# First token group's transposes moved from the second output projection to the third, its operands to the fourth, and the second norm's row scaling moved to GpSimd

## The chip, the cores and the metric

The kernel runs on one core of a Trainium2 chip. The metric is the device time of one execution in microseconds (us), as the median of several runs; lower is better. A core has a matrix engine (TensorE, called PE), a vector engine (DVE), a scalar engine (ACT), GpSimd (POOL) and an engine that here only issues transfers (SP). Each runs its own list of instructions in order, and they wait for one another by semaphores. Sixteen DMA engines carry the transfers.

## The reference

One layer of a decoder: 2048 tokens (T), width 1024 (D), float32.

```python
u = rmsnorm(h, attn_pre_norm)
proj = u @ w_in                                   # 1024 -> 3584 columns, for two groups of heads
o_hg = rmsnorm(hgrn2_mix(q, f, i, lb)) * silu(g)  # gated linear recurrence, 4 heads
o_sb = rmsnorm(stick_breaking_mix(q, k, v))       # causal attention, 8 heads
mix = concatenate([o_hg, o_sb]) @ w_out           # the output projection
h = h + rmsnorm(mix, attn_post_norm)
u = rmsnorm(h, ffn_pre_norm)
gate, up = split(u @ w_gate_up)
h = h + rmsnorm((silu(gate) * up) @ w_down, ffn_post_norm)
h = h + (p @ ple_proj) * sigmoid(h @ ple_gate)
```

`rmsnorm` divides each row (token) by the root of its mean square and multiplies by a gain for each column.

## The kernel before

The tokens are worked in four groups of 512 (`NG`, `GT`), each four blocks of 128 (`TT`, `P`). Every matrix product is done in three passes of a rounded float32 type: an operand is split into a high part (a cast on ACT, L209 for weights, L811 for the FFN) and a low part (a subtraction on DVE or POOL, L210 and L812), and the passes are the lines L223, L224 and L225. The names are `wr` for a raw operand as loaded, `wh` and `wl` for a weight's parts, `uh` and `ul` for the other operand's.

First comes the input projection, under which attention and the recurrence of earlier groups are worked; they end during the second output projection. Attention turns its weights on PE into the PSUM bank "tr" (L443), and DVE and ACT split them (`ah`, `al`, L446, L448); the recurrence multiplies small blocks into the bank "hg" (L525 and others), for which POOL prepares `qp` (L562).

Then come four output projections, `out_proj(0)` to `out_proj(3)`, one for each token group: 32 steps of 12 matmuls, two steps a slot, so that `half` is 8 slots. ACT (L671) and DVE (L673) bring the result into `mix` tiles. `post_mix(g)` follows under the next projection: for each block of 128 tokens it scales `mix` by its norm and gain (L697, DVE), adds the input (L698, POOL), stores the sum `h` (L699), takes the second norm (squares on ACT, L269; row sums and power on POOL, L271, L272, L275), scales the rows by it (L702) and stores them as `un_s[g]` (L703). Then `turn(un_s[g], u_s[g], ...)` transposes this group: it loads tiles `xt` of 128x512 (L730), turns eight groups of four 128x128 blocks on PE into bank "tr" (L745), empties the bank on ACT with the gain into an `ev` buffer (L751), and stores that (L752). The `mix` tiles and the turned tiles share one pool of `ev` buffers, the tiles `xt`, `h` and `gb` one of `xt` buffers.

`first_operands` loads eight turned tiles from `u_s[0]` (L796), and splits them (L811, L812) for the first products of the FFN, which `Drive` runs after the fourth projection.

PE's order is the order in which the program is written: `weave` steps a main stream and, in proportion to its steps, streams beside it. The order on the other engines is chosen when the kernel is built, by a scheduler; the chip keeps to it. All loads and stores are issued by SP, in its order, so what stands behind a transfer that waits, waits too. At most eight transfers are on their way, since a transfer's semaphore is taken again after eight.

Of the kernel before, what the change touches and what calls it, by code (L numbers as in the profile page):

```python
# [12 lines left out]
AF = mybir.ActivationFunctionType  # L13
ALU = mybir.AluOpType
# [4 lines left out]
ND = D // P  # L19
GT = 512  # L20
NG = T // GT
TT = GT // P
# [26 lines left out]
def weave(main, slots, *subs):  # L49
    done = [0] * len(subs)  # L50
    for i in range(2 * slots):
        for k, (sub, total, phase) in enumerate(subs):
            if phase is None or i % 2 == phase:
                due = (i + 1) * total if phase is None else 2 * (i // 2 + 1) * total
                while done[k] * 2 * slots < due:
                    sub.step()
                    done[k] += 1
        main.step()
# [30 lines left out]
def hybrid_block(  # L89
# [6 lines left out]
    nc = tc.nc  # L96
# [8 lines left out]
    def scratch(name, shape):  # L105
        return [dram.tile(list(shape), F32, tag=f"{name}{g}", name=f"{name}{g}") for g in range(NG)]
# [10 lines left out]
    un_s = scratch("un_s", (GT, D))  # L117
    u_s = scratch("u_s", (ND, P, GT))
# [28 lines left out]
    def column(name, src, n):  # L147
        t = ctile(name, (P, n))
        nc.sync.dma_start(t, src.rearrange("(c p) -> p c", p=P))
        return t  # L150

    g_pre = column("g_pre", attn_pre_norm[0], ND)
    g_ffn = column("g_ffn", ffn_pre_norm[0], ND)
# [19 lines left out]
    def bank(tag):  # L173
        return ps.tile([P, 512], F32, tag=tag, name=tag, bufs=BANKS[tag])
# [15 lines left out]
    def xt(name="xt"):  # L190
        return fb.tile([P, GT], F32, tag="xt", name=name, bufs=8)
# [73 lines left out]
    def row_rstd(halves, out=None, ss=None):  # L265
        if ss is None:
            ss = const.tile([P, 2], F32, tag="ss", name="ss", bufs=8)
            for j, y in enumerate(halves):
                nc.scalar.activation(junk, y, AF.Square, accum_out=ss[:, j:j + 1])  # L269
        r = const.tile([P, 1], F32, tag="ssum", name="ssum", bufs=8)  # L270
        nc.gpsimd.tensor_tensor(r, ss[:, 0:1], ss[:, 1:2], op=ALU.add)  # L271
        nc.gpsimd.tensor_scalar(r, r, 1.0 / D, EPS, op0=ALU.mult, op1=ALU.add)  # L272
        if out is None:
            out = const.tile([P, 1], F32, tag="rstd2", name="rstd2", bufs=6)
        nc.gpsimd.tensor_tensor(out, r, neghalf, op=ALU.pow)  # L275
        return out
# [409 lines left out]
    def post_mix(g, mix):  # L686
        gb = [xt("gb") for _ in range(2)]
        for j in range(2):
            nc.sync.dma_start(gb[j], attn_post_norm[0:1][:, j * GT:(j + 1) * GT].to_broadcast((P, GT)))
        for t in range(TT):  # L690
            hs = [xt("h"), xt("h")]
            for j in range(2):
                nc.sync.dma_start(hs[j], x[g * GT + t * P:g * GT + (t + 1) * P, j * GT:(j + 1) * GT])
            r = row_rstd(mix[t])
            for j in range(2):
                d = mix[t][j]
                nc.vector.scalar_tensor_tensor(d, d, r, gb[j], op0=ALU.mult, op1=ALU.mult)  # L697
                nc.gpsimd.tensor_tensor(hs[j], hs[j], d, op=ALU.add)  # L698
                nc.sync.dma_start(h_s[g][t * P:(t + 1) * P, j * GT:(j + 1) * GT], hs[j])  # L699
            r = row_rstd(hs)  # L700
            for j in range(2):
                nc.scalar.activation(mix[t][j], hs[j], AF.Copy, scale=r)  # L702
                nc.sync.dma_start(un_s[g][t * P:(t + 1) * P, j * GT:(j + 1) * GT], mix[t][j])  # L703
            yield

# [17 lines left out]
    def turn(src, dst, gain, tag, new_in, new_out, scales=None):  # L723

        def get(q):
            ts = []
            for i in range(2):
                r = new_in().rearrange("p (t d) -> p t d", t=2)
                rows = src[2 * i * P:2 * (i + 1) * P, q * 256:(q + 1) * 256]
                nc.sync.dma_start(r, rows.rearrange("(t p) d -> p t d", p=P))  # L730
                for n in range(2):
                    if scales:
                        nc.scalar.activation(r[:, n, :], r[:, n, :], AF.Copy, scale=scales[2 * i + n])
                    ts.append(r[:, n, :])
            return ts

        nxt = get(0)
        yield
        for q in range(4):
            ts = nxt  # L740
            nxt = get(q + 1) if q < 3 else None
            for c in range(2):
                b = bank(tag)
                for t in range(TT):
                    nc.tensor.transpose(b[:, t * P:(t + 1) * P], ts[t][:, c * P:(c + 1) * P], ident)  # L745
                e = new_out()
                k = 2 * q + c
                if gain is None:
                    nc.scalar.copy(e, b)
                else:  # L750
                    nc.scalar.activation(e, b, AF.Copy, scale=gain[:, k:k + 1])  # L751
                nc.sync.dma_start(dst[k], e)  # L752
                yield
# [475 lines left out]
    rates = Rate(att_stream, 2, todo, 2 * OP_SLOTS)  # L1229
    r2 = Rate(hgs[2], 1, HG_STEPS - 42, 2)  # L1230
    r3 = Rate(hgs[3], 1, HG_STEPS, 2 * OP_SLOTS - 2)
    half = OP_SLOTS // 2
    tt0, tt1, ss0, ss1 = {}, {}, {}, {}

    def first_operands():
        for prod in (1, 2):
            for k in range(ND // 2):
                t_first(0, tt0, prod, k)
                yield

    for g in range(NG - 1):
        if g + 1 < NG - 1:
            out_load(g + 1, res[g + 1])
        op = Stream(out_proj(g, res[g]))
        if g == 0:
            weave(op, 2, rates.part(2), r2.part(2))
            hgs[2].drain()
            weave(op, OP_SLOTS - 2, rates.part(OP_SLOTS - 2), r3.part(OP_SLOTS - 2))
        elif g == 1:
            weave(op, half, rates.part(half), r3.part(half), (pm, TT, 0))  # L1250
            tu = Stream(turn(un_s[0], u_s[0], g_ffn, "tr", xt, ev))
            weave(op, half, rates.part(half), r3.part(half), (tu, 9, 0))
            hgs[3].drain()
            att_stream.drain()
            side.close()
            big[0] = ctx.enter_context(tc.tile_pool(name="bigr", bufs=1, side="right"))
            mm_tags[:] = ["mm", "z", "mm", "z", "mm", "av"]
        else:
            out_load(NG - 1, res[NG - 1])
            weave(op, half, (pm, TT, 0))  # L1260
            weave(op, half, (Stream(first_operands()), ND, 1))
        op.drain()
        pm = Stream(post_mix(g, res[g]["mix"]))

# [2 lines left out]
    drive.prepare(2)  # L1267
    op = Stream(out_proj(NG - 1, res[NG - 1]))
    tu = Stream(turn(un_s[1], u_s[1], g_ffn, "tr", xt, ev))
    weave(op, half + 2, (pm, TT, 0), (tu, 9, 0))  # L1270

    def third_operands():
        for k in range(ND // 2):
# [75 lines left out]
```

## Time and profile before

| | |
|---|---|
| median of 3 runs | 3080.39 us (3078.42 to 3082.84) |
| the profiled execution | 3079.93 us |
| its span | 3078.1 us |
| granted clock of PE, mean | 0.987 |
| PE busy | 2928.8 us, 95% of the span |
| DVE, ACT, POOL busy | 2042.8, 1580.6, 1603.7 us |
| output projections two to four | 1263 to 1497 us of the span |

An engine's row gives its busy time, its share of the span and its instructions. Where an instruction waited, a row of the timeline ends with the idle time before it and with what released it. A row of the waits sums these: total us, how often, the longest. "issue" stands where the profile shows no releaser. In a row of the transfers stand their count, their size and the median time from issue to landing.

### The profile page before, as it was taken

How to read it: one execution, taken by the hardware profiler on the slowest of the kernel's cores; microseconds unless marked ns; L12 is line 12 of the kernel's file. 1: busy time of each engine (PE TensorE's matmuls, PEld its weight loads, DVE VectorE, ACT ScalarE, POOL GpSimd, SP SyncE). 2: the span in 40 equal slices, each digit the busy share in tenths (PEclk: the TensorE clock that was granted, in tenths of full speed). 3: DMA queues.
4: the chain of work that ended last, by engine and by line, in shares of the span. 5: the costliest groups of instructions: out<-in, count | busy, mean ns of one | idle time of the engine just before them, and what ended most of it. 6: DMA issues, size and time to landing. Idle time of an engine off the chain costs nothing. (4 is left out here: it accounts for less than half of the span.)

```text
span 3078.1 us, 52969 instructions
## 1 busy us (share of the span) xinstructions
PE 2928.8 (95%) x18280; PEld 2429.9 (79%) x18280; DVE 2042.8 (66%) x2809; ACT 1580.6 (51%) x3188; POOL 1603.7 (52%) x1598
## 2 busy tenths in 40 slices
PE   8999999999999998888998999999899999999989
PEld 7888787878787877778776877788788888887767
DVE  3556566677767776745877766856687766656674
ACT  5666656666667666757523233445432323545442
POOL 3344455545556666857454544645634343556564
PEclk9999999999999999999999999999999999999999
DMA  7765565555444443457767767766955555677874
GB/s 216 217 211 164 157 185 158 148 156 162 141 140 150 147 144 122 164 176 264 253 212 245 238 214 236 234 198 218 328 179 171 172 170 175 209 225 251 286 246 144
DMA packets 469421, 602.29 MB, mean 196 GB/s; under 512 B 43168, under 2 KB 277664, under 8 KB 469152
## 3 DMA queue, kind: packets, MB, share of 16 engines
q1 hardware_dynamic: 469152, 598.91, 61.4%
q8 instruction: 144, 2.36, 0.3%
q14 instruction: 125, 1.02, 0.1%
HBM read 439.89 MB, written 158.86 MB: 195 GB/s over the span
## 5 line engine op out<-in xcount | busy, mean ns | idle before, releaser
L811 ACT CAST wh<-wr 128x512 fp32r<-128x512 f32 x600 | 352.3, 618 | 511.1 <-PE mm L224 139.0
L812 POOL TENSOR_TENSOR wl<-wr,wh 128x512 fp32r<-128x512 f32 x256 | 368.7, 1447 | 386.3 <-ACT wh L811 366.8
L435 POOL TENSOR_TENSOR a<-be,ring 128x512 f32<-128x512 f32 (+2 forms) x320 | 318.4, 995 | 434.5 <-DVE ring L431 418.3
L223 PE MATMUL mm<-uh,wh 128*128 128x512 f32 x1168 | 484.5, 415 | 5.2 <-DVE vv L350 3.2
L225 PE MATMUL mm<-uh,wl 128*128 128x512 f32 x1168 | 460.6, 394 | 0.0
L224 PE MATMUL mm<-ul,wh 128*128 128x512 f32 x1168 | 459.0, 393 | 1.6 <-DVE ul L812 1.6
L812 DVE TENSOR_TENSOR wl<-wr,wh 128x512 fp32r<-128x512 f32 x344 | 308.9, 902 | 204.4 <-ACT wh L811 177.6
L431 DVE TENSOR_TENSOR_SCAN ring<-z,ring,be 128x512 f32<-128x512 f32 x192 | 245.6, 1279 | 113.4 <-ACT z L417 110.0
L223 PE MATMUL mm<-wh,uh 128*128 128x256 f32 (+1 forms) x992 | 308.6, 311 | 0.0
L224 PE MATMUL mm<-wl,uh 128*128 128x256 f32 (+1 forms) x992 | 293.4, 296 | 1.6 <-DVE wl L812 1.3
L225 PE MATMUL mm<-wh,ul 128*128 128x256 f32 (+1 forms) x992 | 292.9, 295 | 0.0
L225 PEld LDWEIGHTS mm<-uh,wl 128*128 128x128 f32 x1168 | 220.5, 189 | 51.0
L223 PEld LDWEIGHTS mm<-uh,wh 128*128 128x128 f32 x1168 | 221.4, 190 | 47.6 <-issue 3.3
L224 PEld LDWEIGHTS mm<-ul,wh 128*128 128x128 f32 x1168 | 221.9, 190 | 41.7 <-DVE ul L812 2.0
L448 DVE TENSOR_TENSOR al<-tr,ah 128x512 fp32r<-128x512 f32 (+1 forms) x320 | 192.0, 600 | 90.1 <-ACT ah L446 89.4
L209 ACT CAST wh<-wr 128x512 fp32r<-128x512 f32 x288 | 178.2, 619 | 135.8 <-PE mm L224 81.5
L210 POOL TENSOR_TENSOR wl<-wr,wh 128x512 fp32r<-128x512 f32 x144 | 189.1, 1313 | 98.2 <-ACT wh L209 95.0
L446 ACT CAST ah<-tr 128x512 fp32r<-128x512 f32 (+1 forms) x320 | 167.6, 524 | 110.1 <-PE tr L443 107.1
L416 ACT ACTIVATE be<-z 128x512 f32<-128x512 f32 (+2 forms) x320 | 171.0, 534 | 90.5 <-PE z L410 38.3
L224 PEld LDWEIGHTS mm<-wl,uh 128*128 128x128 f32 x992 | 191.3, 193 | 8.0 <-DVE wl L812 1.7
L223 PEld LDWEIGHTS mm<-wh,uh 128*128 128x128 f32 x992 | 191.0, 193 | 8.1
L225 PEld LDWEIGHTS mm<-wh,ul 128*128 128x128 f32 x992 | 190.7, 192 | 4.3
(305 smaller groups left out, 7285.6 us busy)
## 6 DMA issues: line engine op xcount, KB each, us to landing
wr<-in_w_gate_up_dram SPq DMA_DIRECT2D x308, 256.0 KB, 3.4
wr<-in_w_in_dram SPq DMA_DIRECT2D x224, 256.0 KB, 3.1
wr<-hid_s SPq DMA_DIRECT2D x154, 256.0 KB, 3.1
wr<-in_w_down_dram SPq DMA_DIRECT2D x110, 256.0 KB, 3.3
hid_s<-hs SPq DMA_DIRECT2D x88, 256.0 KB, 2.7
wr<-wd_s SPq DMA_DIRECT2D x88, 256.0 KB, 3.1
kt<-k_s SPq DMA_DIRECT2D x80, 256.0 KB, 3.1
vt<-v_s SPq DMA_DIRECT2D x80, 256.0 KB, 3.3
```

The source lines that it names most:

```text
L209: nc.scalar.copy(hi, src)
L210: (lo_engine or nc.gpsimd).tensor_tensor(lo, src, hi.bitcast(F32), op=ALU.subtract)
L223: nc.tensor.matmul(o, l[0], r[0], start=start, stop=False)
L224: nc.tensor.matmul(o, l[0], r[1], start=False, stop=False)
L225: nc.tensor.matmul(o, l[1], r[0], start=False, stop=stop)
L416: nc.scalar.activation(be[:, :n], z[:, :n], AF.Sigmoid, scale=0.125)
L431: nc.vector.tensor_tensor_scan(r[:, o:o + n][:, ::-1], z[:, :n][:, ::-1], be[:, :n][:, ::-1], init, op0=ALU.mult, op1=ALU.bypass)
L435: nc.gpsimd.tensor_tensor(a[:, :n], be[:, :n], r[:, o + 1:o + n + 1], op=ALU.mult)
L446: nc.scalar.copy(hi[:, lo_c:], tr[:, lo_c:])
L448: nc.vector.tensor_tensor(lo[:, lo_c:], tr[:, lo_c:], hi[:, lo_c:].bitcast(F32), op=ALU.subtract)
L811: nc.scalar.copy(hi, src)
L812: lo_engine.tensor_tensor(lo, src, hi.bitcast(F32), op=ALU.subtract)
```

## The change

It does three things. The scaling of rows in `post_mix`, L702, goes from ACT to POOL (24 instructions of 128x512, in the groups 0 to 2). The first group's `turn` goes from the second half of the second projection to the second half of the third. `first_operands` goes from there to the first ten slots of the fourth projection, beside `post_mix(2)` and `turn(un_s[1])`.

```diff
             r = row_rstd(hs)
             for j in range(2):
-                nc.scalar.activation(mix[t][j], hs[j], AF.Copy, scale=r)
+                nc.gpsimd.tensor_scalar(mix[t][j], hs[j], r, None, op0=ALU.mult)
                 nc.sync.dma_start(un_s[g][t * P:(t + 1) * P, j * GT:(j + 1) * GT], mix[t][j])
...
         elif g == 1:
             weave(op, half, rates.part(half), r3.part(half), (pm, TT, 0))
-            tu = Stream(turn(un_s[0], u_s[0], g_ffn, "tr", xt, ev))
-            weave(op, half, rates.part(half), r3.part(half), (tu, 9, 0))
+            weave(op, half, rates.part(half), r3.part(half))
...
             weave(op, half, (pm, TT, 0))
-            weave(op, half, (Stream(first_operands()), ND, 1))
+            tu = Stream(turn(un_s[0], u_s[0], g_ffn, "tr", xt, ev))
+            weave(op, half, (tu, 9, 0))
...
-    weave(op, half + 2, (pm, TT, 0), (tu, 9, 0))
+    weave(op, half + 2, (pm, TT, 0), (tu, 9, 0), (Stream(first_operands()), ND, 1))
```

What this makes of the engines' lists is shown at three places. On POOL, in the first half of the second projection, before (`h` and `mix` are the tiles of `post_mix`, `rstd` the row scales, `qp` the recurrence's operand):

```order
862 L275 TENSOR_TENSOR rstd_17118<-ssum,neghalf 128x1
863 L698 TENSOR_TENSOR h<-h,mix 128x512
864 L562 TENSOR_TENSOR qp<-qp,tree 128x32x8
865 L698 TENSOR_TENSOR h<-h,mix 128x512
866 L210 TENSOR_TENSOR wl<-wr,wh 128x512
867 L271 TENSOR_TENSOR ssum<-ss 128x1
```

and after:

```order
862 L275 TENSOR_TENSOR rstd_17118<-ssum,neghalf 128x1
863 L702 TENSOR_SCALAR mix<-h,rstd_16927 128x512 x2
864 L698 TENSOR_TENSOR h<-h,mix 128x512 x2
865 L562 TENSOR_TENSOR qp<-qp,tree 128x32x8
866 L210 TENSOR_TENSOR wl<-wr,wh 128x512
867 L435 TENSOR_TENSOR a<-be,ring_217 128x512
```

A pair of scalings, and the second addition, now stand ahead of the `qp` product.

On SP, around the first group's turned tiles: before, their eight reloads stand together in the third projection's first half, all of the stores being long issued:

```order
910 L616 DMA tmp_18160<-o_s3_6_143 128x512
911 L796 DMA wr_18607<-u_s0_99 128x512
912 L796 DMA wr_18640<-u_s0_99 128x512
913 L796 DMA wr_18685<-u_s0_99 128x512
914 L796 DMA wr_18718<-u_s0_99 128x512
915 L796 DMA wr_18763<-u_s0_99 128x512
```

and after, in its second half (`un_s0` and `u_s0` are the first group's rows and turned tiles):

```order
918 L752 DMA u_s0_99<-ev_18511 128x512
919 L699 DMA h_s1_88<-h_18306 128x512
920 L699 DMA h_s1_88<-h_18307 128x512
921 L796 DMA wr_18947<-u_s0_99 128x512
922 L730 DMA xt_18502<-un_s0_95 128x2x256
923 L730 DMA xt_18504<-un_s0_95 128x2x256
924 L752 DMA u_s0_99<-ev_18562 128x512
925 L703 DMA un_s1_96<-mix_16705 128x512
926 L730 DMA xt_18592<-un_s0_95 128x2x256
927 L796 DMA wr_18992<-u_s0_99 128x512
```

Each reload (L796) now stands close behind the store that it reads (L752), and loads of `xt` stand behind it.

On ACT, in the third projection's second half, before:

```order
1841 L209 CAST wh_18818<-wr_18816 128x512
1842 L671 ACTIVATE mix_18578<-z_18750,rg_18215 128x256
1843 L671 ACTIVATE mix_18579<-z_18750,rg_18215 128x256
1844 L209 CAST wh_18824<-wr_18822 128x512
1845 L671 ACTIVATE mix_18580<-mm_18783,rg_18215 128x256
1846 L671 ACTIVATE mix_18581<-mm_18783,rg_18215 128x256
1847 L209 CAST wh_18972<-wr_18970 128x512
```

and after:

```order
1801 L751 ACTIVATE ev_18562<-tr_18557,g_ffn_172 128x512
1802 L811 CAST uh_18949<-wr_18947 128x512
1803 L209 CAST wh_18612<-wr_18610 128x512
1804 L209 CAST wh_18692<-wr_18690 128x512
1805 L671 ACTIVATE mix_18516<-mm_18565,rg_18135 128x256
1806 L671 ACTIVATE mix_18517<-mm_18565,rg_18135 128x256
1807 L811 CAST uh_18994<-wr_18992 128x512
1808 L751 ACTIVATE ev_18601<-tr_18596,g_ffn_172 128x512
1809 L269 ACTIVATE junk_204,ss_18420<-h_18402 128x512
1810 L209 CAST wh_18698<-wr_18696 128x512
```

Evictions (L751) and casts of reloaded operands (L811) now stand between the weight casts. Here `ev_18562` and `mix_18516` take buffers whose last contents went out with the store of the eviction just before, and wait until that has landed.

## The prediction

> **What bounds the kernel now.** I read the head of the page first, then the busy time by stretches, then what the TensorE (PE) waited for in each stretch, and last the timelines around those waits.
>
> ```profile
> span 3078.1 us, 52969 instructions
> PE 2928.8 (95%) x18280; PEld 2429.9 (79%) x18280; DVE 2042.8 (66%) x2809; ACT 1580.6 (51%) x3188; POOL 1603.7 (52%) x1598
> ```
>
> PE is busy for 95% of the span, so an edit counts only where PE idles or where it makes PE idle. The profiled execution took 3079.93 us, 1.83 us more than its span and 0.46 us below the median of 3080.39; my sum is made against 3079.93, and the median differs by less than can be told apart.
>
> The stretches are: first projection (1176:1250, for comparison), both halves of the second (1264:1313, 1313:1375), both halves of the third (1376:1403, 1403:1436), and the part of the fourth in which the second group is turned (1436:1470). Columns: length, busy time of each engine with its count, granted clock, DMA share, GB/s.
>
> ```profile
> 1176.00:1250.00 74.00, 71.13 (x906) 63.81 (x906) 50.99 (x82) 47.36 (x105) 45.89 (x56) 1.00 0.35 110
> 1264.00:1313.00 49.00, 40.50 (x466) 35.73 (x466) 34.84 (x51) 37.51 (x88) 43.31 (x56) 0.93 0.54 181
> 1313.00:1375.00 62.00, 51.18 (x575) 46.87 (x574) 27.98 (x48) 30.76 (x61) 29.66 (x34) 0.97 0.48 154
> 1376.00:1403.00 27.00, 22.64 (x180) 21.63 (x179) 21.33 (x24) 24.24 (x53) 23.06 (x25) 1.00 0.99 333
> 1403.00:1436.00 33.00, 29.43 (x231) 28.82 (x230) 18.89 (x25) 17.38 (x40) 21.74 (x25) 0.95 0.60 199
> 1436.00:1470.00 34.00, 29.47 (x242) 28.39 (x241) 13.18 (x20) 25.93 (x59) 23.50 (x31) 1.00 0.87 305
> ```
>
> PE idles 8.5 us of the 49, 10.8 of the 62, 4.4 of the 27, 3.6 of the 33 and 4.5 of the 34. What it waited for (total us, times, longest), in the same stretches:
>
> ```profile
> PE hg L525 <- POOL qp L562: 6.1, 2, 4.0
> ...
> PE tr L745 <- issue: 6.6, 3, 3.0
> PE tr L745 <- DVE al L448: 3.3, 2, 1.7
> ...
> PE tr L443 <- ACT ev L751: 0.2, 1, 0.2
> ...
> PE tr L745 <- ACT ev L751: 4.4, 3, 1.6
> ```
>
> So the transposes that the change moves (L745) hold 9.9 of the 10.8 us in the second projection's second half: they share the PSUM bank "tr" with attention's own transposes L443, and wait for that bank. In the first half the bound is POOL, 43.31 busy of 49. The same transposes in the fourth projection wait for ACT to empty the bank.
>
> **The change, term by term.**
>
> A. Second projection, second half: eight groups of L745 go. One group costs PE 0.35 us without a wait, from its start to that of the next matmul:
>
> ```profile
> 1357.38 0.60 PE L745 MATMUL tr<-ident,xt 128*128 128x128 f32 x4
> 1357.73 0.36 PE L223 MATMUL mm<-wh,uh 128*128 128x256 f32 x1
> ...
> 1358.05 0.28 PE L225 MATMUL mm<-wh,ul 128*128 128x256 f32 x1
> 1358.17 0.28 PE L223 MATMUL mm<-wh,uh 128*128 128x256 f32 x1
> ```
>
> Removed: waits 6.6 + 3.3 + 0.2 = 10.1, work 8 x 0.35 = 2.8, and about 1.0 of the slow clock (0.97 on 51 us of work is at most 1.5). Put back: with shorter cover, attention will hold PE as it does in the first projection, 2.87 idle of 74; on the 48 us that are left that is 1.9, against 0.7 of other idle time now, so +1.2. A = -12.7. ACT (30.76 less 8 evictions) and POOL (29.66) still fit into 48 us, so I put the ends at -14 and -8.
>
> B. Second projection, first half: POOL gets 8 scalings L702 of 128x512. POOL has not run this one; its nearest row is another TENSOR_SCALAR of that size, beside the ACT row that goes (least, median, most ns):
>
> ```profile
> L507 POOL TENSOR_SCALAR pd<-pd,oml,lb x16: 767/776/1209, 219.2 to 1282.6; 128x512 f32<-128x512 f32 x16
> ...
> L702 ACT ACTIVATE mix<-h,rstd x24: 705/720/757, 1272.9 to 1472.5; 128x512 f32<-128x512 f32 x24
> ```
>
> 8 x 0.78 = 6.2 us on an engine that has 5.7 idle and on which PE already waits. The pairs stand in POOL's queue right ahead of the qp products (L562) for which PE waits twice, so a pair, 1.55, is added to each: +3.1. Ends: 0, if POOL's idle time takes them, and +6.2, if all are in front of qp. ACT loses 5.8 of 37.51 there, but no long wait names it, so I count nothing.
>
> C. Third projection, first half: POOL gets another 6.2 on 23.06 of 27. But the first operands leave: eight loads, eight ACT casts L811 and eight DVE subtractions L812, which here run beside POOL and stretch it. Rows of DVE and of POOL:
>
> ```profile
> 1389.26 3.43 DVE L812 TENSOR_TENSOR ul<-wr,uh 128x512 fp32r<-128x512 f32 x2
> ...
> 1385.35 3.44 POOL L698 TENSOR_TENSOR h<-h,mix 128x512 f32<-128x512 f32 x2 [1.31 <-DVE mix L697]
> ...
> 1445.32 1.27 POOL L698 TENSOR_TENSOR h<-h,mix 128x512 f32<-128x512 f32 x1 [2.21 <-PE z L225]
> ```
>
> A POOL product takes 1.72 beside DVE and 1.27 alone. About four of POOL's products meet L812, so 4 x 0.45 = 1.8 comes back and POOL stands at 23.06 + 6.2 - 1.8 = 27.5 of 27: full, while ACT, DVE and the DMA (0.99) ease. C = +0.5, ends -3 (the easing wins) and +4.4 (6.2 - 1.8, all of it late).
>
> The Trainium skill ("SBUF — State Buffer", Terms) says that VectorE and GpSimd share one port pair by an exclusive lock, on which the loser stands fully blocked for the whole instruction; the rule speaks against moving work to POOL, and by it all 24 scalings could hold DVE or be held. The trace agrees in part: 1.72 against 1.27 is a loss of 0.45, not of a whole instruction. It gives the third rival below.
>
> D. Third projection, second half: eight groups of turn(un_s[0]) come in. Their bank is free of attention here, but ACT's order is now eviction, store, cast of a reloaded operand (L811), next eviction: most evictions take an `ev` buffer whose store must have landed first, five of them the store of an eviction just before. The half now lasts from 1402.79 to 1432.49, 29.7 us:
>
> ```profile
> 1402.79 0.28 PE L225 MATMUL mm<-wh,ul 128*128 128x256 f32 x1
> ...
> 1432.49 0.28 PE L225 MATMUL mm<-wh,ul 128*128 128x256 f32 x1
> 1408.84 0.58 PE L224 MATMUL z<-wl,uh 128*128 128x256 f32 x1 [2.81 <-POOL wl L210]
> 1416.80 0.39 PE L224 MATMUL av<-wl,uh 128*128 128x256 f32 x1 [0.68 <-POOL wl L210]
> ```
>
> If all of the turn were hidden it would last 29.7 + 2.8 - 3.5 (both waits hidden too) = 29.0. By the chain it lasts: 3.0 until the first xt load, which stands in SP's queue behind stores that now wait for POOL (estimate: a pair of L702 and half a landing), 8 evictions x 0.69 = 5.5, some four other ACT rows of 0.62 between them, 2.5, six landings in series, and after the last group 24 matmuls x 0.12 = 2.9. That is 13.9 + six landings. A landing of 256 KB (KB, median us), in 1320:1375, 1400:1436 and 1436:1470:
>
> ```profile
> u_s<-ev SPq DMA_DIRECT2D x8, 256.0 KB, 3.8
> ...
> h_s<-h SPq DMA_DIRECT2D x5, 256.0 KB, 3.0
> ...
> u_s<-ev SPq DMA_DIRECT2D x8, 256.0 KB, 5.2
> ...
> 1446.61 0.66 PE L745 MATMUL tr<-ident,xt 128*128 128x128 f32 x4 [1.30 <-ACT ev L751]
> ```
>
> With 3.8 it is 36.7, D = +7.0; with 3.0, 31.9 and +2.2; with 5.2, 45.1 and +15.4. I take 3.8: it is the same transfer, at a DMA share of 0.48, and the 0.60 of this half grows by some 20 transfers, while the queue, which stops at each store, keeps few in flight. In the fourth projection, where the buffers are two evictions apart, PE waits 4.4 for such a turn; here they are one apart. The ends are -0.7 and +15.4.
>
> The Trainium skill ("DMA: Bandwidth & Descriptors", Anatomy of one DMA) fits a transfer on the GpSimd path by 2.0 us and bytes over 436 GB/s; for 256 KB that is 2.6 (an estimate; these stores are issued by SP). By it D would be -0.2 and the whole sum -6.7. The medians above, 3.0 to 5.2, lie higher.
>
> E. Fourth projection: the last two operands' casts stand on ACT ahead of the weight cast (L209) of the second product, each behind a store and a reload, 2 x 3.8 = 7.6, of which one product of 3 us (24 matmuls) is cover: +4.6. Against it, eight L702 leave ACT (5.8 of 25.93), which should halve the 4.4 of waits for evictions: -2.0, estimated. E = +2.6, ends -3 and +6. The casts and subtractions that come here run on a DVE with 13.18 of 34 busy, so they are hidden. POOL, 23.50 + 6.2 of 34, stays under its length.
>
> Sum: -12.7 + 3.1 + 0.5 + 7.0 + 2.6 = +0.5, so 3079.93 + 0.5 = 3080.4.
>
> **The rivals.** First, the gain is kept. Landings at 2.6 to 3.0 hide the chain (D about +1), POOL's idle time takes half of the scalings (B +1.5), the eased DMA and ACT win in C (-1), E is 0: -12.7 + 1.5 - 1 + 1 = -11.2, 3069. For it: A rests on waits that are plainly in the rows, and 3.0 is what stores take in this very stretch. Against it: PE waits for just such evictions in the fourth projection.
>
> Second, slower: the chain through `ev` and DMA decides alone. If the added transfers fill the DMA as in 1436:1470 (share 0.87), a landing is 5.2, D = +15.4, E = +4.6: -12.7 + 3.1 + 0.5 + 15.4 + 4.6 = +10.9, 3091. It costs more than A gives from landings of about 4.7 on. For it: the same store at 5.2 one stretch later. Against it: a queue that waits for landings cannot keep the engines full.
>
> Third, slower by POOL: each scaling is stretched as L698 is, 0.78 + 0.45 = 1.23, 9.8 a half. Then the first halves run at POOL's length: B = 43.31 + 9.8 - 49 = 4.1, and the 3.1 for the order as well, C = 23.06 + 9.8 - 1.8 - 27 = 4.1: -12.7 + 7.2 + 4.1 + 7.0 + 2.6 = +8.2, 3088. For it: L507 once took 1.209. Against it: its median of 0.776, in stretches as busy as these.
>
> **How the numbers follow.** 0.2%, 6.2 us, is about what a measurement of this kernel can tell from no change. My forecast, within it, gets 0.38; the gain kept 0.34; the chain 0.18; POOL 0.10. So faster 0.34, same 0.38, slower 0.28. The likeliest alone spans 3074 to 3086; the range takes in the kept gain and the chain: 3067 to 3092.
>
> **What would show it.** Right: no L745 among the waits of the second projection's second half, which shrinks from 61 to about 48.5 us; L525 waiting for qp for over 6.1 us in its first half; L745 waiting for `ev` L751 for some 7 us or more in the third projection's second half, and that half at about 37 us; L702 on POOL at a median near 0.78. Wrong: a second half of the third projection at 30 us (then the first rival), landings there over 4.7 (the second), L702 near 1.2 (the third), or another stage that loses by more than 3 us, the FFN's start above all, for which I count nothing.

## Result, and the profile after

The changed kernel takes 3096.82 us (median of 6 runs, 3089.08 to 3100.52) against 3079.40 for the kernel before: ratio 1.0057, interval 1.0040 to 1.0073. It is slower by 0.57% and lies above the range of 3067 to 3092. The profiled execution took 3095.75 us. The head of its page:

```profile
span 3093.9 us, 52956 instructions
PE 2938.6 (95%) x18280; PEld 2438.3 (79%) x18280; DVE 2035.6 (66%) x2809; ACT 1569.5 (51%) x3164; POOL 1636.7 (53%) x1622
```

POOL gained 33 us of busy time, ACT lost 11: the 24 scalings cost POOL far more than the 18.7 us of the prediction. The stretches of the changed kernel are both halves of the second projection, the third projection up to one matmul of its second quarter (L224, at 1398.25 here and at 1399.69 before), its rest, and the fourth (length, busy time by engine, granted clock, DMA share, GB/s):

```profile
1266.10:1317.30 51.20, 39.47 (x457) 34.93 (x457) 33.54 (x51) 33.64 (x81) 49.64 (x56) 0.90 0.57 185
1317.30:1368.80 51.50, 48.97 (x550) 45.05 (x550) 27.99 (x48) 25.38 (x54) 33.06 (x40) 0.97 0.32 105
1368.80:1398.30 29.50, 22.43 (x167) 21.38 (x166) 16.55 (x20) 19.26 (x44) 28.12 (x28) 0.92 0.59 192
1398.30:1442.90 44.60, 36.00 (x259) 34.57 (x260) 15.27 (x24) 21.97 (x47) 24.20 (x26) 0.90 0.84 276
1442.90:1510.10 67.20, 55.90 (x427) 54.67 (x426) 32.52 (x48) 37.17 (x86) 46.77 (x54) 0.92 0.88 298
```

The kernel before, cut at the same instructions (the windows are rounded, by up to 0.4 us):

```profile
1263.00:1311.00 48.00, 39.53 (x456) 34.76 (x456) 33.53 (x51) 37.36 (x89) 42.97 (x55) 0.93 0.55 183
1311.00:1374.00 63.00, 51.80 (x577) 47.50 (x578) 28.58 (x50) 31.15 (x62) 29.68 (x35) 0.97 0.47 151
1374.00:1400.00 26.00, 21.64 (x172) 20.63 (x172) 20.93 (x24) 23.43 (x52) 23.09 (x24) 1.00 1.00 340
1400.00:1432.60 32.60, 29.03 (x227) 28.42 (x226) 17.88 (x25) 19.00 (x42) 20.93 (x26) 0.95 0.67 219
1432.60:1490.50 57.90, 52.34 (x427) 50.66 (x426) 29.75 (x45) 38.91 (x88) 31.04 (x39) 1.00 0.89 312
```

POOL is busy for 49.64 of 51.20 and 28.12 of 29.50 us in the first and third of these stretches: it is the bound there. The second projection's second half did shrink, by 11.5 us. The third and fourth projections give back 25: 13.5 of it is more idle time of PE, 2.8 the transposes that came in, and some 8.5 longer busy time of the same matmuls (114.3 us against 103.0, less the 2.8). The lower granted clocks explain nearly all of that: the busy time of before, rescaled stretch by stretch to the clocks of after, grows by 8.0. What PE waited for in the five stretches of the changed kernel:

```profile
PE hg L525 <- POOL qp L562: 8.9, 2, 7.2
...
PE hg L589 <- DVE sl L585: 2.2, 1, 2.2
...
PE z L224 <- POOL wl L210: 3.5, 2, 2.5
...
PE tr L745 <- ACT ev L751: 6.0, 3, 3.0
PE tr L745 <- DMA xt<-un_s: 2.5, 3, 1.3
...
PE z L224 <- POOL wl L210: 7.3, 3, 3.5
PE tr L745 <- DVE rg L643: 3.1, 1, 3.1
```

And the group of L702 (least, median, most ns):

```profile
L702 POOL TENSOR_SCALAR mix<-h,rstd x24: 1563/1576/2522, 1279.2 to 1496.2; 128x512 f32<-128x512 f32 x24
```

One scaling costs POOL 1.576 us, not 0.78, and no single one of the 24 took less than 1.563. How that meets PE is seen in the second projection's first half; rows of POOL's timeline, then of PE's:

```profile
1277.91 1.30 POOL L210 TENSOR_TENSOR wl<-wr,wh 128x512 fp32r<-128x512 f32 x1
1279.18 3.76 POOL L702 TENSOR_SCALAR mix<-h,rstd 128x512 f32<-128x512 f32 x2
1282.91 1.09 POOL L435 TENSOR_TENSOR a<-be,ring 128x512 f32<-128x512 f32 x1
1283.96 2.48 POOL L698 TENSOR_TENSOR h<-h,mix 128x512 f32<-128x512 f32 x2
1286.43 0.76 POOL L507 TENSOR_SCALAR pd<-pd,oml,lb 128x512 f32<-128x512 f32 x1
...
1287.95 0.66 PE L525 MATMUL hg<-qp,ks 128*32 128x32 f32 x32 [7.25 <-POOL qp L562]
```

PE waits from 1280.70 to 1287.95. The pair of scalings takes 3.76 us, 2.2 of them inside this wait; the rest of the wait is the rows behind it, up to the `qp` product. L507, the row from which the price was taken, takes 0.76 three rows on.

That pair ran beside work of DVE. In the rest of the third projection two scalings ran with DVE idle but for one row; POOL's row, then DVE's:

```profile
1412.46 3.13 POOL L702 TENSOR_SCALAR mix<-h,rstd 128x512 f32<-128x512 f32 x2
...
1414.92 0.69 DVE L812 TENSOR_TENSOR ul<-wr,uh 128x512 fp32r<-128x512 f32 x1 [6.88 <-ACT uh L811]
```

DVE sat idle for 6.88 us until 1414.92, so the first of the two, which ended at 1414.04, had nothing beside it and still took 1.58 us.

### The profile page after: what moved, and what is told of

Same layout as the page of the kernel before. It is cut to its first block, busy times and chain, and to the rows that moved or that the text cites. A ratio compares the mean times of both kernels' runs of the same rounds, so it can differ in the third digit from the quotient of the medians.

```text
span 3093.9 us, 52956 instructions
## 1 busy us (share of the span) xinstructions
PE 2938.6 (95%) x18280; PEld 2438.3 (79%) x18280; DVE 2035.6 (66%) x2809; ACT 1569.5 (51%) x3164; POOL 1636.7 (53%) x1622
## 3 DMA queue, kind: packets, MB, share of 16 engines
q1 hardware_dynamic: 469152, 598.91, 61.5%
## 5 line engine op out<-in xcount | busy, mean ns | idle before, releaser
L811 ACT CAST wh<-wr 128x512 fp32r<-128x512 f32 x600 | 352.5, 618 | 512.4 <-PE mm L224 135.6
L812 POOL TENSOR_TENSOR wl<-wr,wh 128x512 fp32r<-128x512 f32 x256 | 365.9, 1436 | 387.2 <-ACT wh L811 371.8
L224 PE MATMUL mm<-ul,wh 128*128 128x512 f32 x1168 | 459.8, 394 | 2.7 <-DVE ul L812 2.7
L812 DVE TENSOR_TENSOR wl<-wr,wh 128x512 fp32r<-128x512 f32 x344 | 310.8, 909 | 203.5 <-ACT wh L811 182.9
L224 PE MATMUL mm<-wl,uh 128*128 128x256 f32 (+1 forms) x992 | 295.1, 297 | 3.6 <-DVE wl L812 2.9
L224 PEld LDWEIGHTS mm<-ul,wh 128*128 128x128 f32 x1168 | 222.2, 190 | 42.9 <-DVE ul L812 3.1
L210 POOL TENSOR_TENSOR wl<-wr,wh 128x512 fp32r<-128x512 f32 x144 | 188.7, 1310 | 99.2 <-ACT wh L209 94.0
L224 PEld LDWEIGHTS mm<-wl,uh 128*128 128x128 f32 x992 | 193.1, 195 | 9.9 <-DVE wl L812 3.4
```

What stands on the lines that cost most here:

```text
L210: (lo_engine or nc.gpsimd).tensor_tensor(lo, src, hi.bitcast(F32), op=ALU.subtract)
L224: nc.tensor.matmul(o, l[0], r[1], start=False, stop=False)
L811: nc.scalar.copy(hi, src)
L812: lo_engine.tensor_tensor(lo, src, hi.bitcast(F32), op=ALU.subtract)
```

## Experiments

Lengths of the stages in each profiled execution, in us, cut at the L640 sums that open each projection, the first L589 of the recurrence's last head, the L224 of the third projection named above, the first matmul of the FFN, and the FFN's first long wait of L745. The last column is what comes after. Each row is one execution, up to 7 us off the median of its kernel, so differences of one or two us in a cell mean little.

| kernel | second, first half | second, second half | third, first part | third, rest | fourth | FFN's start | rest |
|---|---|---|---|---|---|---|---|
| before | 48.0 | 63.0 | 25.3 | 32.9 | 57.9 | 193.8 | 1393.8 |
| changed | 51.2 | 51.5 | 29.5 | 44.7 | 67.2 | 192.5 | 1391.3 |
| e1_moves | 48.0 | 48.4 | 30.9 | 34.9 | 64.9 | 191.1 | 1391.9 |
| e2_pool | 52.9 | 74.2 | 27.5 | 31.6 | 64.6 | 194.3 | 1392.4 |
| e3_two_ops | 53.4 | 48.4 | 29.4 | 38.5 | 62.2 | 191.6 | 1396.9 |
| e4_pool_two_ops | 53.3 | 63.9 | 30.2 | 33.7 | 61.7 | 191.1 | 1391.6 |
| e7_own_bank | 50.6 | 51.2 | 24.8 | 34.9 | 57.5 | 193.9 | 1392.2 |
| e10_both_acc | 49.1 | 48.3 | 31.7 | 32.1 | 57.2 | 1579.2 with the rest | |
| e13_counter | 48.1 | 48.4 | 30.9 | 35.8 | 64.2 | 190.6 | 1386.2 |
| e15_acc_no_count | 49.1 | 48.3 | 30.9 | 32.5 | 63.1 | 196.5 | 1388.8 |
| e16_late_weights | 47.9 | 48.3 | 25.2 | 40.0 | 66.3 | 190.6 | 1398.1 |
| e17_own_bank_late | 49.1 | 51.2 | 25.8 | 32.5 | 55.7 | 192.1 | 1384.0 |
| e18_changed_late | 52.4 | 49.9 | 25.4 | 44.4 | 64.9 | 195.0 | 1393.3 |

All ratios below are to the kernel before, run on the same chip.

### The two parts of the change, and the scaling's form

**The moves alone** (e1_moves):

```diff
-                nc.gpsimd.tensor_scalar(mix[t][j], hs[j], r, None, op0=ALU.mult)
+                nc.scalar.activation(mix[t][j], hs[j], AF.Copy, scale=r)
```

> The two moves alone: the second norm's scaling L702 is back on ACT, the transposes and the first operands stay where the change puts them. Theory P (POOL's price): the loss of the changed kernel comes from L702 costing POOL 1.576 us each instead of the 0.78 that I took, so without it the first halves of the second and third projections fall back to about 48 and 25 us, the fourth projection to about 60, and the time is 3066 to 3075, clearly under the kernel before. Theory R (round trips): the loss comes from the chain eviction, store, reload and cast; then the third projection's second half stays at about 44 us and the fourth at about 65, only some 7 us come back, and the time is 3084 to 3092.

Measured: 3078.56 us, ratio 0.9981 (0.9968 to 0.9995). The moves alone gain a little: 14.7 us in the second half of the second projection, of which the third and fourth take back 14.6 in this execution. Theory P's number was too low and theory R's too high; the sign is P's. Read against this row of the table, the scaling on POOL costs the changed kernel 3.2, 3.1, -1.4, 9.8 and 2.3 us in the five stages, 17.0 in all.

**The scaling alone** (e2_pool: the kernel before with the line of the change on POOL):

> The scaling alone: L702 on POOL, transposes and operands where they were before. Theory P: 24 x 1.576 = 38 us of POOL time fall into halves in which it is already full; the second projection's first half grows by 3, the third's first half by 4 or more (its first operands still run there), the fourth by 5 to 9; with the second half of the second projection unchanged the time is 3092 to 3102. Theory R: only the two first halves lose, 3 to 7 in all, and the time is 3082 to 3087.

Measured: 3098.63, ratio 1.0041 (1.0024 to 1.0059). Alone it loses about 13 us, so it is the scaling that makes the change slower. In the profiled execution, the slowest of the eight and 6 us above their median, 11 us of the loss lie where neither theory put them, in the second projection's second half: the transposes wait there for loads of the rows that POOL has scaled. The group, and PE's longest wait from the halves' border on:

```profile
L702 POOL TENSOR_SCALAR mix<-h,rstd x24: 1551/1572/2448, 1280.2 to 1508.1; 128x512 f32<-128x512 f32 x24
...
PE tr L745 <- DMA xt<-un_s: 6.4, 1, 6.4
```

**The changed kernel, scaling in two operations** (e3_two_ops):

```diff
-                nc.gpsimd.tensor_scalar(mix[t][j], hs[j], r, None, op0=ALU.mult)
+                nc.gpsimd.tensor_scalar(mix[t][j], hs[j], r, 1.0, op0=ALU.mult, op1=ALU.mult)
```

> The changed kernel with L702 written as two operations, times the row's scale and times 1.0, the form in which POOL's other scaling of this size, L507, took 0.776. If the form sets the price, L702 falls from 1.576 to about 0.78; theory P then expects 3066 to 3080, theory R 3086 to 3094. If L702 stays at 1.58, the price hangs on something else (input and output being different tiles, or neighbours), and the time stays at 3094 to 3100 by both.

Measured: 3085.03, ratio 1.0003 (0.9991 to 1.0015).

```profile
L702 POOL TENSOR_SCALAR mix<-h,rstd x24: 687/692/1380, 1281.3 to 1480.8; 128x512 f32<-128x512 f32 x24
```

A second operation, a multiplication by one, makes the instruction 2.3 times as fast: 0.692 against 1.576 us. The form sets the price. With it the loss against the kernel before is gone. Of the 0.76% by which the changed kernel stands above the moves alone, the form is 0.54, and 0.22 remain as the cost of the cheap form on POOL. Stage by stage the rest of the third projection is 6.2 and the fourth 5.0 shorter than in the changed kernel, the second half of the second 3.1; only its first half did not get shorter (53.4), at a granted clock of 0.84. The scheduler answered the new form with another order (41 of POOL's 1622 instructions stand elsewhere), so a part of the gain may be the order's; no run parts the two.

**The scaling alone, in two operations** (e4_pool_two_ops):

> The scaling alone, on POOL, as two operations; transposes and operands as before. If the price falls to 0.78, theory P expects half or less of the loss of the scaling alone, 3080 to 3088; theory R 3078 to 3084. If the price stays at 1.58, the time equals that of the scaling alone in one operation.

Measured: 3092.45, ratio 1.0026 (1.0014 to 1.0039), L702 at 0.692 at the median. Nearly two thirds of the loss remain at a price below that of ACT's 0.720, more than P expected, though the two intervals overlap. In the profiled execution the cheap form costs 5.3 us in the second projection's first half and 4.9 in the third's first part. In the whole third projection PE waits 11.8 us for low parts of weights from POOL (L210), against 6.4 before. POOL itself is busy for 47.7 of the 53.3 us of that first half, so it is late there without being full.

### Where the moves lose what they gain

**The operands later** (e5_late_operands: the moves alone, `first_operands` from the first ten slots of the fourth projection to its last six):

> The two moves alone (scaling on ACT), and the first operands still later: in the last six slots of the fourth projection, behind the second group's transposes. With the moves alone the third projection took 65.8 us and the fourth 64.9, against 58.2 and 57.9 before. Theory O (reloads and casts of the operands, waiting among the evictions, cost these 14.6 us): the third falls to 60 or less, the fourth to 60 or less unless the loads at its end hold the FFN back; time 3068 to 3075. Theory V (the evictions wait for buffers of `ev` whatever stands between them): both stay within 2 us, time 3076 to 3082.

Measured: 3078.62, ratio 0.9980 (0.9968 to 0.9991), third 67.7 and fourth 62.5. No change in the time: theory O falls.

**Tiles of their own** (e6_acc_tiles):

```diff
-            tu = Stream(turn(un_s[0], u_s[0], g_ffn, "tr", xt, ev))
+            tu = Stream(turn(un_s[0], u_s[0], g_ffn, "tr", xt, acc))
```

> The two moves alone, but the first group's turned tiles go to the FFN's `acc` buffers (two, used by nothing else there) instead of the pool that they share with the `mix` tiles. Theory V: evictions no longer wait for stores of `mix`, and two buffers take turns, so the third projection falls from 65.8 to about 61 and the fourth by a few; time 3068 to 3076. Theory O: the casts still wait for the reloads; third and fourth stay within 2 us, time 3076 to 3082.

Measured: 3066.55, ratio 0.9939 (0.9926 to 0.9951): the time that V expected, but not from where V expected it. The third projection took 64.7, the fourth 61.5, and what comes after the FFN's start 1384.8, against 65.8, 64.9 and 1391.9 with the moves alone. The edit had a second effect: `acc` deals its tiles to two pools by a counter, which eight tiles more leave at another place for the whole FFN. Two runs part the two effects.

**The counter alone** (e13_counter: the moves alone, with `turns["acc"] += 8` ahead of the FFN):

> The two moves alone (scaling on ACT), with the counter that deals the FFN's `acc` buffers to their two pools advanced by 8 before the FFN: buffers are given out in another order, all work is the same. If the counter is what gained after the FFN's start when the turned tiles went to `acc`, this gains about 4 to 6 on the moves alone (ratio to the kernel before 0.9960 to 0.9970, from 0.9981) and the third and fourth projection stay at 65.8 and 64.9. If the shared buffers are the cause, it stays at 0.998.

Measured: 3069.69, ratio 0.9964 (0.9952 to 0.9976).

**Tiles of their own, the counter set back** (e15_acc_no_count: `turns["acc"] -= 8` ahead of the FFN):

> The two moves with the first group's turned tiles in `acc`, the counter set back by 8 before the FFN, so that its buffers are dealt as in the kernel before. If the counter made the gain after the FFN's start, the FFN's start is as with the moves alone and the ratio 0.9955 to 0.9968; if the buffers did, 0.9939 again. Theory V for the third and fourth projection expects 64.7 and 61.5 us again.

Measured: 3075.14, ratio 0.9979 (0.9967 to 0.9991), third 63.4, fourth 63.1. The counter gains; buffers of their own, by themselves, gain nothing that shows in the time. The counter's gain lies in the FFN. From its first matmul to the end, the twelve kernels without the shift (the one before and the changed one among them) take 1582 to 1589 us in their profiled executions, the seven with a shift of 8 take 1566 to 1578. The shift changes the order of the engines' lists as well, so "counter" stands for both.

The two parts do not add up to the whole: 0.0017 and 0.0002 against 0.0042 for the tiles in `acc`. And theory V does not fall with the time: with the tiles in `acc` and the counter set back, the rest of the third projection and the fourth together are 4.2 us shorter than with the moves alone, but the FFN's start is 5.4 longer; its long wait of L745 is 16.0 us there, and 12.1 with the moves alone. Why is not shown.

**The FFN's weights later** (e16_late_weights: the moves alone, `drive.prepare(2)` moved behind the fourth projection's first ten slots). With the moves alone, 5.6 us are lost in the third projection's first part. PE's waits there, and POOL's rows ahead of the longest:

```profile
PE av L224 <- POOL wl L210: 5.4, 1, 5.4
...
1374.70 3.45 POOL L698 TENSOR_TENSOR h<-h,mix 128x512 f32<-128x512 f32 x2 [0.63 <-DVE mix L697]
1378.10 1.72 POOL L628 TENSOR_TENSOR oss<-oss,tmp 128x512 f32<-128x512 f32 x1
1379.78 1.72 POOL L812 TENSOR_TENSOR wl<-wr,wh 128x512 fp32r<-128x512 f32 x1
1381.46 1.71 POOL L210 TENSOR_TENSOR wl<-wr,wh 128x512 fp32r<-128x512 f32 x1
```

The scheduler has filled the room that the operands left with the FFN's weights (L812), ahead of the weight for which PE waits.

> The two moves alone, with the FFN's first weights prepared (loads, casts L811, subtractions L812) in the fourth projection's last slots instead of ahead of it. With the moves alone PE waited 5.4 us for a weight's low part that stood on POOL behind such a subtraction, two L698 and L628. Theory W (these weights, drawn forward, cost it): the wait goes to about 1, the third projection falls from 65.8 to about 60, and unless the FFN's start then waits for its weights, the ratio to the kernel before is 0.996 to 0.9965. Rival (POOL is full there whatever stands in which order): the third projection stays at 64 or more, ratio 0.998.

Measured: 3077.40, ratio 0.9982 (0.9973 to 0.9991). The long wait for POOL goes, as W said; the longest is now one of 2.43 us, for DVE:

```profile
1368.76 0.39 PE L224 MATMUL z<-wl,uh 128*128 128x256 f32 x1 [0.76 <-POOL wl L210]
1375.77 0.39 PE L224 MATMUL av<-wl,uh 128*128 128x256 f32 x1 [2.43 <-DVE wl L210]
```

In the third projection's first part W is right: it falls from 30.9 to 25.2 us, the 25.3 of the kernel before. The three kernels of the table with these weights late (e16, e17, e18) take 25.2 to 25.8 there, those with the moves and the weights early 29.4 to 31.7. (The scaling alone on POOL, with the operands still in this part, takes 27.5 and 30.2.) But the rest of the projection takes 40.0 instead of 34.9, where PE waits 4.9 us for evictions and loads of the transposes (2.6 with the moves alone), and the fourth 66.3. So the total does not move, and what lengthens the rest is not shown.

**The changed kernel with these weights late** (e18_changed_late):

> The changed kernel (scaling on POOL in one operation) with the FFN's first weights late. Theory P: POOL's price stays, so at most 4 to 6 us come back, 1.0035 to 1.0045. If the weights were the larger part of the loss, 1.002 or less.

Measured: 3096.61, ratio 1.0043 (1.0026 to 1.0060): the price stays, as P said, and within the intervals nothing comes back. The third projection's first part is back at 25.4 us here too, with the scaling still on POOL, while its rest stays at 44.4. So the 4.2 us that the changed kernel lost in the first part are these weights, and not the scaling; the scaling's cost lies behind it.

**The scaling on DVE** (e8_dve: the changed kernel with `nc.vector.tensor_scalar`):

> The changed kernel with the second norm's scaling on DVE instead of POOL. DVE is busy 33 of 51 us, 28 of 52, 16 of 29 and 15 of 45 in the four halves. If only POOL was full, the second projection's first half is back at 48 and the third and fourth are as with the moves alone or, ACT being relieved of 17 us, shorter: 3070 to 3077. Rival: DVE, one operation of which meets POOL's, makes both later, and the first half stays above 50: 3080 to 3086.

Measured: 3079.23, ratio 0.9982 (0.9972 to 0.9991), L702 at 0.480. The first half of the second is back at 49.2, the third took 69.1, the fourth 60.4. The time equals that of the moves alone (third 65.8, fourth 64.9): that ACT is relieved of the scalings is worth nothing in the time.

### The gain without the loss

**Another bank** (e7_own_bank: the kernel before, one word changed):

```diff
-            tu = Stream(turn(un_s[0], u_s[0], g_ffn, "tr", xt, ev))
+            tu = Stream(turn(un_s[0], u_s[0], g_ffn, "mm", xt, ev))
```

> The kernel before, with one edit: the first group's transposes, still in the second projection's second half, go to the PSUM banks `mm` of the projection instead of the bank `tr` that attention uses. If sharing that bank is what cost the 9.9 us of waits there, the half falls from 63 to about 53 and nothing else moves: 3070 to 3073. Rival: the transposes wait instead for the projection's own banks, or for their loads (three of the waits showed no releaser), and the half stays at 60 or more: 3078 to 3086.

Measured: 3071.65, ratio 0.9953 (0.9940 to 0.9967). All that PE waits for over 0.2 us in that half now, and the half itself:

```profile
PE hg L589 <- DVE sl L585: 1.0, 1, 1.0
PE hg L604 <- POOL acc L597: 0.7, 1, 0.7
...
1314.20:1365.40 51.20, 50.52 (x581) 46.71 (x582) 28.70 (x48) 30.89 (x63) 30.06 (x36) 1.00 0.60 187
```

No L745 waits; the half falls from 63.0 to 51.2 with the transposes still in it, and the third and fourth projections stay as they were, within 2 us. Hardly anything else differs: POOL's list has the same order, and two instructions of ACT and one of DVE stand elsewhere. `tr` is a single bank in this kernel and `mm` three that are used in turn, so the transposes still share, but no longer wait. It was the shared bank, not the place in the program.

**With the second group's tiles in `acc`** (e9_bank_acc):

> The kernel before with the first group's transposes in the banks `mm` (3071.7 alone, 12 us under before), and with the second group's turned tiles in the `acc` buffers instead of those that the `mix` tiles use. If the evictions' waits for stores of `mix` (4.0 us of PE's waits in the fourth projection) go, 3066 to 3069; if two buffers are too few for a turn that goes beside `post_mix`, 3072 to 3076.

Measured: 3058.62, ratio 0.9936 (0.9922 to 0.9950).

**With the counter's shift instead** (e14_bank_counter):

> The kernel before with the first group's transposes in the banks `mm`, and the same shift of the counter; the second group's turned tiles stay with the `mix` tiles. With those in `acc` it was 0.9936, without 0.9953. If the counter made the difference, 0.9936 to 0.9942; if the buffers did, 0.9953.

Measured: 3062.04, ratio 0.9938 (0.9921 to 0.9956). Equal to the one above: what that gained is the counter's shift. (Both intervals overlap with that of the other bank alone; the FFN's length parts them, 1577 and 1578 us with the shift against 1586.)

**And the FFN's weights late** (e17_own_bank_late: e9_bank_acc with `drive.prepare(2)` moved):

> The fastest version (transposes in the banks mm, second group's turned tiles in acc, 0.9936), with the FFN's first weights late as well. In it, as in the kernel before, only one of these subtractions runs in the third projection's first half, so theory W expects a gain of 2 us at most there: 0.993 to 0.9936; if the FFN's start waits for them, 0.9945 or more.

Measured: 3059.88, ratio 0.9923 (0.9909 to 0.9938), the lowest ratio of all; its interval overlaps that of e9_bank_acc.

**Three more combinations.** Both groups' tiles in `acc` (e10_both_acc):

> The two moves alone with the first group's turned tiles in `acc` (3066.6), and the second group's as well. PE waits 1.5 us for evictions of the first and 3.0 of the second there. If buffers of `ev` are the cause of the latter, 3062 to 3065; if ACT's order is, no change, 3065 to 3069.

Measured: 3065.58, ratio 0.9954 (0.9940 to 0.9968). The counter goes on by 16 here, and no run has that shift alone, so the time does not part the two. The stages do show the buffers. PE's waits for evictions in the third and in the fourth projection, with the moves alone and here:

```profile
PE tr L745 <- ACT ev L751: 2.6, 1, 2.6
PE tr L745 <- ACT ev L751: 5.5, 2, 3.5
...
PE tr L745 <- ACT acc L751: 1.1, 1, 1.1
PE tr L745 <- ACT acc L751: 0.3, 1, 0.3
```

The rest of the third projection and the fourth fall from 34.9 and 64.9 to 32.1 and 57.2 us, about what they took before the change (32.9 and 57.9); the shift of the counter alone, by 8, left them at 35.8 and 64.2. So in this execution what the moves lose there is lost for want of `ev` buffers, as theory V says. The first part, where the weights stand, stays at 31.7.

The changed kernel in two operations with the first group's tiles in `acc` (e11_two_ops_acc):

> The changed kernel with L702 on POOL as two operations (3085.0), and the first group's turned tiles in `acc`. Theory V (evictions wait for `ev` buffers, and more so behind stores that wait for POOL): PE's waits for xt loads and evictions in the third projection fall by 4 or more and the FFN's start gains as with the scaling on ACT, 3070 to 3076. If POOL alone keeps this kernel back, it gains 5 or less: 3080 to 3085.

Measured: 3070.47, ratio 0.9970 (0.9956 to 0.9983), from 1.0003. About half is the counter's shift (0.0017 with the moves alone); what the rest is was not parted.

POOL in two operations for two groups of three (e12_mixed: as e6_acc_tiles, L702 on ACT for the first group alone):

> The two moves with the first group's turned tiles in `acc` (3066.6), and L702 on POOL as two operations for the second and third group alone, on ACT for the first, under whose post_mix POOL is 43 of 49 us busy. If POOL's cost lies in the second projection's first half alone (+5 us there when all 24 are on POOL), this gains what ACT loses in work, 3062 to 3066; if POOL is as full in the third projection's first half (24 of 27), 3067 to 3073.

Measured: 3062.62, ratio 0.9944 (0.9925 to 0.9964), the same as with all on ACT.

## Why the prediction was wrong, step by step

The step that failed is the price of L702, "8 x 0.78 = 6.2 us", which stands in the terms B, C and E. It was taken from L507, a TENSOR_SCALAR of the same size and engine but with two operations; with one it takes 1.576, so that the eight scalings of a group cost POOL 12.6 us and more. Against the moves alone this scaling costs 17.0 us in the stages; the sum had +3.1 for it in B and +0.5 in C. The highest price that the prediction weighed, 1.23 in the third rival, came from a stretching beside DVE, and was no bound for another form.

The run in two operations puts 0.692 in place of 1.576 and measures 1.0003 (0.9991 to 1.0015), which is +0.9 us where the sum said +0.5. So the price is the step that carried the miss. That the rest of the sum then fits so well is in part luck: in that run's profile the terms are -14.7 (A), +5.4 (B), +9.7 (C and D, for +7.5) and +4.3 (E), each about two us off and partly against one another.

- **A** (-12.7): -11.5 in the changed kernel, -14.7 with the scaling on ACT. Right, for the reason given; the run with another bank shows it to be the bank. The 3.1 between them belong to the scaling: its last pair of the first group slipped into this half.
- **B** (+3.1): +3.2. The number hit with a price half of the true one; at 0.692 it is +5.4 and +5.3, at granted clocks of 0.84 and 0.90, against 0.93 before. That PE would wait longer for qp was right (8.9 us for 6.1); the size of the step was luck.
- **C** (+0.5): +4.2, near the end that I gave it for all of POOL's work coming late, but not for that reason. POOL is busy for 28.12 of 29.50 and bounds the stretch, yet only two of the group's eight scalings ran in it (4.1 us), and six behind it; in the kernel before it is four and four, so "another 6.2" was misread. What came in is the FFN's weights, drawn forward into the room that the operands left: with them late the stretch is back at 25.4 with the scaling on POOL, and at 25.2 with it on ACT. No term had them. The rows shown for the stretching do not overlap in time (L698 ends at 1388.79, L812 begins at 1389.26); of the POOL rows that do meet L812 there, the L628 take 1.73 and 1.75 and one L210 1.28.
- **D** (+7.0): +11.8, but only +2.0 with the scaling on ACT, no more than kernels without the moves vary there (32.5 to 34.9 us in the table). The chain was sized too high, and 9.8 are the scaling's. The chain itself is in the trace: ACT's rows wait for stores and reloads, and SP for stores.

```profile
1417.39 0.47 ACT L671 ACTIVATE mix<-mm,rg 128x256 f32<-128x256 f32 x1 [1.06 <-DMA u_s<-ev]
...
1420.56 0.62 ACT L811 CAST uh<-wr 128x512 fp32r<-128x512 f32 x1 [1.76 <-DMA wr<-u_s]
1421.29 0.69 ACT L751 ACTIVATE ev<-tr,g_ffn 128x512 f32<-128x512 f32 x1
...
SPq L796 <- DMA u_s<-ev: 6.2, 6, 2.0
...
u_s<-ev SPq DMA_DIRECT2D x8, 256.0 KB, 4.0
```

The landing of 4.0 is the 3.8 that I took. PE waits 6.0 us for the evictions, a little under the "7 us or more", and 2.5 for loads. The buffers that I blamed cost little here: with tiles of their own and the scaling on ACT the stretch takes 32.1 and 32.5 us, with shared ones 34.9. Where they cost is the fourth projection (E). The reloads can go without a change of the time (e5_late_operands). By which of these waits the scaling's 9.8 us come in was not parted; POOL is busy for only 24.20 of 44.60 us there, so it is late and not full. I did not count the clock either: apart from the transposes the same matmuls took some 4 us longer, of which the granted clock, 0.90 against 0.95, explains less than half.
- **E** (+2.6): +9.3; +7.0 with the scaling on ACT, +4.3 in two operations. Mis-sized. The waits in the changed kernel are not the operands' casts but weights that POOL is late with (7.3 us, from 1.0), at a POOL busy 46.77 instead of 31.04, the bank "tr", which DVE is late to empty of the projection's sums (L643, 3.1 us), and the clock (0.92 from 1.00, 3.6 us). With the scaling on ACT they are waits for evictions (5.5 us), and with tiles of their own for both groups the fourth is at 57.2. The relief of ACT, -2.0, did not show: the run on DVE has it, and its time equals that of the moves alone.
- **The rivals.** The third, slower by POOL, had the right term, the wrong mechanism and 0.10; it stopped at 1.23 us a scaling and 3088. A stretching beside DVE is not what made the price: it is 1.58 us with DVE idle. The stretching is real all the same: in two operations five of the 24 scalings took 1.10 to 1.38 us, all of them beside DVE's work, at a median of 0.692.

What stays open: with the scaling on ACT, the moves still lose 14.6 us in the third and fourth projections (in the profiles, 6.7 of it idle time of PE, 2.8 the transposes and about 5 the clock). Weights late give back the 5.6 of the first part, and tiles of their own for both groups the 9.0 behind it, each in one profiled execution; the first lengthens the rest again, and the two were not tried together. Why the counter's shift is worth 5 us in the FFN was not traced either.

## What to carry to other kernels

Price an added instruction from a row of the same form, operations and operands included, not only of the same name and size; where there is none, the bound has to reach well beyond the slowest row of the other form. Before work is moved to escape a wait, look at what it waits for: here it was a second user of one PSUM bank, and one changed word did what the move had done, at no price that shows. An edit that draws from a shared dealer of buffers also changes what everyone after it gets; shift the dealer alone before the edit is believed. And where an edit does not move the time, look at the stages: here a gain in one was twice eaten by the next.

## What the runs showed of the hardware

GpSimd's TENSOR_SCALAR on 128x512 float32 takes 1.576 us (1.551 to 2.522 in two kernels) with one operation and 0.692 us (0.682 to 1.777 in two kernels) with two, the second a multiplication by 1.0; L507, two operations with a column each, 0.776. The Trainium skill ("GPSIMD Engine Reference", Performance versus the Vector engine) gives 769 ns for 512 elements as the best case. The least of L507, 0.767, agrees. L702 with two operations lies under it, at 0.692, so that 769 is not the best case here; with one operation it lies at twice that, and the page does not tell the two apart.

Several stretches in which PE waits had the lower granted clock: 0.90 to 0.92 in the third and fourth projections of the changed kernel, in which PE idles 27 of 141 us, and 1.00 in the half with the transposes in `mm`, in which PE idles 0.7 of 51.2 us. The Trainium skill ("TensorE: Matmul & The Clock Gate", Part 1) says that the default is a throttled clock and that activity releases it. The trace agrees in tendency alone: the kernel before has 1.00 in a stretch (1374:1400) in which PE idles 4.4 of 26 us.
